# Holding back the preparation of weights until the first token tile is normalised: at three layer-norm boundaries the run-ahead of a weight queue gets a limit

## The chip, the cores and the metric

One core of a Trainium2 chip runs the whole kernel. The metric is the device time of one execution in microseconds; the figure quoted is the median of several runs. The engines are TensorE (PE, the matrix products; PEld its weight loads), VectorE (DVE), ScalarE (ACT), GpSimd (POOL) and SyncE (SP, which here only issues DMAs). Each engine works through its own list of instructions in order and waits at an instruction until the semaphores that it names have been reached.

## The reference

A decoder block of one layer works on 256 tokens of width 2048: a SwiGLU feed-forward net (width 5632), a mixer (recurrence plus attention), a second SwiGLU net, and a gated projection of per-layer embeddings. Behind each of the first three parts stands a residual and a layer norm over the 2048 columns of a token.

```python
def swiglu(x, w_gate, w_up, w_down):
    return (jax.nn.silu(x @ w_gate) * (x @ w_up)) @ w_down

x = layer_norm(ALPHA * x + 0.5 * swiglu(x, ffn1...), ln1_g, ln1_b)
x = layer_norm(ALPHA * x + hybrid_mixer(x, ...),     ln2_g, ln2_b)   # mixer: ... @ w_out
x = layer_norm(ALPHA * x + 0.5 * swiglu(x, ffn2...), ln3_g, ln3_b)
x = x + sigmoid(x @ w_ple_gate) * (p @ w_ple_proj)
```

All matrices are float32, so every weight passes through the core once, in 413 MB of transfers.

## The kernel before, in words

**Weights as entries of a plan.** A list `plan` holds all weights in the order of use, as entries of 256 rows by 512 columns (512 KB). An entry goes through three steps. SP loads it into a tile `raw` (10 buffers). ACT rounds it to a high part `hi` (line 104). DVE subtracts to get the low part `lo` (line 109). A product is then three passes on TensorE: act-high by hi, act-high by lo, act-low by hi.

**Where hi and lo live.** Most entries use the pools `whi` and `wlo` of 7 buffers each. An entry with `"work": True` takes both its tiles from the common pool `work` of 11 buffers (names `w4_...`, shown as `w` in the profile), which also holds activations. Such entries are the third and fourth of the eight that end each of the three parts (`last_down`), and the first three of the part that follows. At the end of a part the pool holds the two halves of the activations (2 tiles), the third and fourth entries (4 tiles), and what of the next part's first three entries is prepared (up to 6 tiles). In front of the third boundary one more tile holds the split per-layer embeddings.

**What sets the order.** `take()` hands out the next entry and lets `advance()` prepare further ones, up to 7 ahead (`AHEAD`), at most to `self.limit`, and only while fewer than 7 slots (`SLOTS`) of `whi` are in use; entries in the work pool don't count. `advance_lo` lets the subtractions lag the casts by one entry. `done(e)` gives a slot back and calls `advance()` again. No scheduler reorders anything within an engine: the order in which Python makes these calls is the order on each engine. Semaphores are added where a buffer is written again, so an instruction that needs a buffer waits for its last reader.

**The boundary.** `down_last` is the end of each part; it runs three times, at about 690, 1061 and 1770 us. It makes the last four column groups of 512 columns for the first token tile (tokens 0 to 127, below t0), two entries each. DVE adds each bank to `acc` (line 385) and takes its statistics (line 513). `ln_norm` then joins the statistics (lines 518 and 520), lets GpSimd take the inverse root (line 522), and scales the four column groups (line 525). The same four column groups follow for the second token tile (t1) with the same eight entries. In the middle of its second group, after 18 of the 48 matmuls of t1, stand the first transposes of the normalised t0 (`ln_transpose`, line 535). They are followed by ACT (lines 538 and 64) and DVE (line 65), which make the next part's activations `xT`. The next part starts with t0 for eight entries, and the transposes of t1 stand inside that.

**Names.** Below, the three calls are boundary I, II and III. The eight entries of `down_last` are e0 to e7 (e2 and e3 in the work pool). The entries of the next part are v0, v1, v2 (work pool), v3, and so on.

Of the kernel before, what the change touches and what calls it, by code (L numbers as in the profile page):

```python
# [40 lines left out]
class Block:  # L41
# [449 lines left out]

    def down_last(self, acts):
        es, st = [], [self.tile(self.small, [P, 4, 6], F32, "bst") for _ in range(2)]
        for n in range(4):
            es.append([self.take(), self.take()])
            self.down_mm(acts, es[n], 0, n, False)
            self.ln_stats(st[0], 0, n)
        self.ln_norm(st[0], 0)
        for n in range(4):
            self.down_mm(acts, es[n], 1, n, False, mid=(lambda: self.ln_transpose(0, 0)) if n == 1 else None)  # L500
            self.ln_stats(st[1], 1, n)
            if n < 3:
                for e in es[n]:
                    self.done(e)
            if n > 0:
                self.ln_transpose(0, n)
        self.ln_norm(st[1], 1)
        for e in es[3]:
            self.done(e)
# [499 lines left out]
```

## Time and profile before

| | us |
|---|---|
| median of 3 runs (1910.5 to 1912.78) | 1912.32 |
| the profiled execution's own time | 1905.79 |
| its span, first to last instruction | 1904.0 |
| PE busy | 1868.5 (98%) |
| DVE busy | 1494.9 (79%) |
| ACT busy | 1077.8 (57%) |

The profiled execution is another one than the three timed, and 6.5 us shorter than their median. PE is busy nearly all the time, so what can be won lies in the short stretches in which it stands still or runs at a lower clock. The page averages over stages; a boundary of some 20 us does not show in it, and has to be looked up in the timeline.

### The profile page before, as it was taken

The numbers are of one execution on the slowest core, as the hardware profiler recorded it, in microseconds if no ns is written. First come the engines' busy times: TensorE is split into PE (matmuls) and PEld (weight loads), VectorE is DVE, ScalarE is ACT, GpSimd is POOL, SyncE is SP. The second block draws the span as 40 slices with busy tenths as digits, with TensorE's granted clock in tenths as the row PEclk, the third lists the DMA queues.
The fourth block names the chain that finished last, engine by engine and source line by source line (L and its number), as shares of the span: only waits on it lengthen the run. The fifth ranks groups of instructions, "written<-read, shape, count | busy, mean of one in ns | idle before, by whom it ended". The sixth has DMA issues, their size and how long they took to land.

```text
span 1904.0 us, 26424 instructions
## 1 busy us (share of the span) xinstructions
PE 1868.5 (98%) x9844; PEld 1603.2 (84%) x9844; DVE 1494.9 (79%) x1910; ACT 1077.8 (57%) x1422; POOL 124.2 (7%) x108
## 2 busy tenths in 40 slices
PE   8999999999999989999999899999999999999899
PEld 7888888888888878887888788888888888888687
DVE  6698887887888876688677867878879888788674
ACT  6565555555655646555755455655556556556552
POOL 0001010100010000011100000101000101010000
PEclk9999999999999999999999999999999999999999
DMA  9678687788786857565455575887887878778381
GB/s 354 232 198 264 203 257 235 207 260 247 211 255 209 266 178 231 175 185 158 138 184 187 167 243 155 250 231 211 258 247 207 255 211 253 243 198 276 131 263 44
DMA packets 214593, 413.02 MB, mean 217 GB/s; under 512 B 13104, under 2 KB 15808, under 8 KB 214464
## 3 DMA queue, kind: packets, MB, share of 16 engines
q1 hardware_dynamic: 193856, 370.42, 58.1%
q0 software_dynamic: 20608, 40.91, 12.6%
q8 instruction: 77, 1.26, 0.3%
q14 instruction: 52, 0.43, 0.1%
HBM read 409.18 MB, written 2.10 MB: 216 GB/s over the span
## 4 chain that ended last, share of the span: by engine, by line
PE 95%; DVE 2%; ACT 1%; issue 1%; DMA 0%; SPq 0%; POOL 0%; DVEq 0%; POOLq 0%; ACTq 0%
PE mm L264 94%; DVE lo L109 1%; PE mm L535 1%; DMA raw<-in_ffn_w_gate_dram 0%; ACT hi L104 0%; DVE w L109 0%; DVE bst L513 0%; DVE acc L385 0%; PE mm L792 0%; DVE raw L82 0%; DVE w L721 0%; DVE w L65 0%; ACT w L64 0%; POOL rs L522 0%; DVE w L627 0%
## 5 line engine op out<-in xcount | busy, mean ns | idle before, releaser
L104 ACT CAST hi<-raw 128x1024 fp32r<-128x1024 f32 (+1 forms) x774 | 797.2, 1049 | 556.4 <-PE mm L264 501.2
L264 PE MATMUL mm<-xT,hi 128*128 128x512 f32 x3072 | 1057.6, 391 | 5.6 <-ACT hi L104 5.6
L109 DVE TENSOR_TENSOR lo<-raw,hi 128x1024 fp32r<-128x1024 f32 (+1 forms) x774 | 915.2, 1221 | 93.4 <-ACT hi L104 84.5
L264 PE MATMUL mm<-xT,lo 128*128 128x256 f32 x3072 | 850.5, 277 | 0.1
L264 PEld LDWEIGHTS mm<-xT,hi 128*128 128x128 f32 x3072 | 577.5, 188 | 127.2 <-ACT hi L104 5.8
L264 PEld LDWEIGHTS mm<-xT,lo 128*128 128x128 f32 x3072 | 577.7, 188 | 6.3 <-DVE lo L109 1.3
L264 PE MATMUL mm<-hi,w 128*128 128x512 f32 x1480 | 481.6, 391 | 1.8 <-DVE acc L435 1.2
L264 PEld LDWEIGHTS mm<-hi,w 128*128 128x128 f32 x1480 | 277.9, 188 | 63.7 <-ACT hi L104 1.5
L264 PE MATMUL mm<-lo,w 128*128 128x512 f32 x740 | 289.5, 391 | 0.0
L264 PE MATMUL mm<-hi,xT 128*128 128x512 f32 (+1 forms) x648 | 200.9, 385 | 0.0
L264 PEld LDWEIGHTS mm<-lo,w 128*128 128x128 f32 x740 | 139.1, 188 | 23.9
L85 POOL DMA_DIRECT2D raw<-in_ffn_w_down_dram x72 | 86.6, 1214 | 1080.7 <-DVE raw L82 547.7
L437 DVE TENSOR_TENSOR acc<-acc,mm 128x512 f32<-128x512 f32 x110 | 75.2, 684 | 98.6 <-PE mm L264 98.6
L264 PEld LDWEIGHTS mm<-hi,xT 128*128 128x128 f32 x648 | 120.3, 188 | 23.1
L264 PE MATMUL mm<-lo,xT 128*128 128x512 f32 (+1 forms) x324 | 123.6, 382 | 0.0
L378 DVE TENSOR_TENSOR w<-mm,w 128x256 f32<-128x256 f32 x192 | 80.2, 419 | 20.5 <-ACT w L377 20.0
L82 DVE TENSOR_TENSOR raw<-raw,raw 128x1024 f32<-128x1024 f32 x72 | 87.9, 1221 | 1.2
L377 ACT COPY w<-mm 128x256 f32<-128x256 f32 x192 | 69.6, 364 | 21.2 <-PE mm L264 17.2
L64 ACT CAST w<-qk 128x512 fp32r<-128x512 f32 (+1 forms) x42 | 25.5, 609 | 86.4 <-DVE qk L482 46.0
L612 ACT ACTIVATE w<-w 128x256 f32<-128x256 f32 x84 | 35.1, 418 | 66.3 <-DVE w L378 66.3
L264 PEld LDWEIGHTS mm<-lo,xT 128*128 128x128 f32 x324 | 61.0, 188 | 11.2
L613 DVE TENSOR_TENSOR w<-w,w 128x256 f32<-128x256 f32 x84 | 35.8, 426 | 41.4 <-ACT w L612 41.4
(139 smaller groups left out, 788.0 us busy)
## 6 DMA issues: line engine op xcount, KB each, us to landing
raw<-in_ffn_w_up_dram SPq DMA_DIRECT2D x176, 512.0 KB, 4.9
raw<-in_ffn_w_down_dram SPq DMA_DIRECT2D x176, 512.0 KB, 5.3
raw<-in_ffn_w_gate_dram SPq DMA_DIRECT2D x175, 512.0 KB, 6.0
raw<-in_w_in_dram SPq DMA_DIRECT2D x88, 512.0 KB, 4.6
raw<-in_ffn_w_down_dram POOLq DMA_DIRECT2D x72, 512.0 KB, 7.6
raw<-in_w_out_dram SPq DMA_DIRECT2D x32, 512.0 KB, 4.4
raw<-in_w_ple_gate_dram SPq DMA_DIRECT2D x32, 512.0 KB, 5.6
w<-in_ln_g_dram SPq DMA_DIRECT2D x12, 256.0 KB, 7.4
```

The lines of the kernel that those rows point to most:

```text
L64: self.nc.scalar.copy(hi, src)
L82: self.nc.vector.tensor_tensor(a, a, b, op=ALU.add)
L85: self.nc.gpsimd.dma_start(a, src, accum_op=ALU.add)
L104: self.nc.scalar.copy(e["hi"][:, k, :], e["raw"][:, k, :])
L109: self.nc.vector.tensor_tensor(e["lo"][:, k, :], e["raw"][:, k, :], e["hi"][:, k, :].bitcast(F32), op=ALU.subtract)
L264: self.nc.tensor.matmul(out, lhsT=lhsT, rhs=rhs, start=start, stop=stop, skip_group_check=True)
L377: self.nc.scalar.copy(c, bank[:, 256:])
L378: self.nc.vector.tensor_tensor(dst, bank[:, :256], c, op=ALU.add)
L437: self.nc.vector.tensor_tensor(a, a, bank, op=op)
L535: nc.tensor.transpose(bank[:, q * P:(q + 1) * P], self.acc[:, t, kb * P:(kb + 1) * P], self.ident)
L612: nc.scalar.activation(s, g, AF.Sigmoid)
L613: nc.vector.tensor_tensor(g, g, s, op=ALU.mult)
```

## The change

`down_last` sets the limit of the run-ahead to its own eight entries and two more before the first token tile, and lifts it again behind that tile's `ln_norm`. All other code stays.

```diff
     def down_last(self, acts):
         es, st = [], [self.tile(self.small, [P, 4, 6], F32, "bst") for _ in range(2)]
+        self.limit = self.taken + 10
         for n in range(4):
             es.append([self.take(), self.take()])
             self.down_mm(acts, es[n], 0, n, False)
             self.ln_stats(st[0], 0, n)
         self.ln_norm(st[0], 0)
+        self.limit = len(self.plan)
         for n in range(4):
             self.down_mm(acts, es[n], 1, n, False, mid=...)
             self.ln_stats(st[1], 1, n)
             if n < 3:
                 for e in es[n]:
                     self.done(e)
```

After the limit is lifted, the next call of `advance()` is the one in `done` behind the first column group of t1. The instructions of PE, ACT, SP and POOL stand in the same order as before, apart from buffer numbers. Only on DVE do some move, in the same way at each boundary. Place 1 is DVE at boundary I, from the statistics of the first column group to those of the last (`mm` are the four banks of t0, `w4_1283`, `w4_1287` and `w4_1290` the low parts of v0, v1 and v2). Before:

```order
L513 BN_STATS bst_1276_6561<-acc_85 128x6 [waits DVE_49]
L109 TENSOR_TENSOR w4_1283_6572<-raw_1267_6505,w4_1282_6571 128x1024 [waits DMAHW3_49,Activation_49]
L109 TENSOR_TENSOR w4_1287_6593<-raw_1270_6523,w4_1286_6592 128x1024 [waits DMAHW4_49,Activation_49]
L385 TENSOR_TENSOR acc_85<-acc_85,mm_1291_6602 128x512 [waits PE_49]
L513 BN_STATS bst_1276_6561<-acc_85 128x6 [waits DVE_49]
L109 TENSOR_TENSOR w4_1290_6599<-raw_1273_6541,w4_1289_6598 128x1024 [waits DMAHW5_49,PE_49,Activation_49]
L385 TENSOR_TENSOR acc_85<-acc_85,mm_1295_6623 128x512
L513 BN_STATS bst_1276_6561<-acc_85 128x6 [waits DVE_49]
L385 TENSOR_TENSOR acc_85<-acc_85,mm_1296_6638 128x512
L513 BN_STATS bst_1276_6561<-acc_85 128x6 [waits DVE_49]
```

The same place with the change (two lines were added, so lines behind 494 carry higher numbers):

```order
L515 BN_STATS bst_1276_6561<-acc_85 128x6 [waits DVE_49]
L109 TENSOR_TENSOR w4_1283_6572<-raw_1267_6505,w4_1282_6571 128x1024 [waits DMAHW3_49,Activation_49]
L385 TENSOR_TENSOR acc_85<-acc_85,mm_1288_6596 128x512 [waits PE_49]
L515 BN_STATS bst_1276_6561<-acc_85 128x6 [waits DVE_49]
L385 TENSOR_TENSOR acc_85<-acc_85,mm_1289_6611 128x512 [waits PE_49]
L515 BN_STATS bst_1276_6561<-acc_85 128x6 [waits DVE_49]
L385 TENSOR_TENSOR acc_85<-acc_85,mm_1290_6626 128x512 [waits PE_49]
L515 BN_STATS bst_1276_6561<-acc_85 128x6 [waits DVE_49]
```

The subtractions for v1 and v2 are gone from it. The one for v2 was the one that waits for PE.

Place 2 is DVE at boundary I behind the normalisation of t0, from the addition of t1's first bank to the first low part of `xT`. Before:

```order
L385 TENSOR_TENSOR acc_85<-acc_85,mm_1300_6663 128x512
L513 BN_STATS bst_1277_6562<-acc_85 128x6 [waits DVE_49]
L109 TENSOR_TENSOR lo_1294_6620<-raw_1278_6563,hi_1293_6619 128x1024 [waits DMAHW6_49,Activation_49]
L109 TENSOR_TENSOR lo_1303_6681<-raw_1281_6569,hi_1302_6680 128x1024 [waits DMAHW7_49,Activation_49]
L65 TENSOR_TENSOR xT_84<-qk_1309_6698,xT_84 128x4x128 [waits Activation_49]
```

The same place with the change:

```order
L385 TENSOR_TENSOR acc_85<-acc_85,mm_1294_6651 128x512 [waits PE_49]
L515 BN_STATS bst_1277_6562<-acc_85 128x6 [waits DVE_49]
L109 TENSOR_TENSOR w4_1287_6593<-raw_1270_6523,w4_1286_6592 128x1024 [waits DMAHW4_49,Activation_49]
L109 TENSOR_TENSOR w4_1297_6669<-raw_1273_6541,w4_1296_6668 128x1024 [waits DMAHW5_49,PE_49,Activation_49]
L109 TENSOR_TENSOR lo_1300_6675<-raw_1278_6563,hi_1299_6674 128x1024 [waits DMAHW6_49,Activation_49]
L109 TENSOR_TENSOR lo_1303_6681<-raw_1281_6569,hi_1302_6680 128x1024 [waits DMAHW7_49,Activation_49]
L67 TENSOR_TENSOR xT_84<-qk_1309_6698,xT_84 128x4x128 [waits Activation_49]
```

The two subtractions now stand here, ahead of those for v3 and v4 and of the first low part of `xT`.

Place 3 is PE at boundary I in t1's second column group, the same before and after. `w4_1260` and `w4_1261` are hi and lo of e2; the last row is the first transpose.

```order
L264 MATMUL mm_1307_6690<-w4_1260_6467,w4_1192_6125 128x512
L264 MATMUL mm_1307_6690<-w4_1261_6468,w4_1192_6125 128x512
L264 MATMUL mm_1307_6690<-w4_1260_6467,w4_1193_6126 128x512
L264 MATMUL mm_1307_6690<-w4_1260_6467,w4_1192_6125 128x512
L264 MATMUL mm_1307_6690<-w4_1261_6468,w4_1192_6125 128x512
L264 MATMUL mm_1307_6690<-w4_1260_6467,w4_1193_6126 128x512
L535 MATMUL mm_1308_6697<-ident_86,acc_85 128x128 [waits DVE_49]
```

Nothing moved here. The fifth row is the last reader of `w4_1261`; it is this matmul that the subtraction for v2 waits for, before and after, as its own low part takes that buffer.

## Rows read from the trace of the kernel before

**Rows 1.** Waits over the whole span: total us, times, longest

```profile
DVE w L109 <- PE mm L264: 13.2, 2, 6.9
PE mm L535 <- DVE acc L525: 19.1, 3, 8.0
```

**Rows 2.** Timeline of PE, boundary I: start us, us, instructions, idle before

```profile
688.63 2.88 PE L264 MATMUL mm<-w,w 128*128 128x512 f32 x12
...
699.51 1.52 PE L264 MATMUL mm<-w,w 128*128 128x512 f32 x6
706.62 1.11 PE L535 MATMUL mm<-ident,acc 128*128 128x128 f32 x4 [5.59 <-DVE acc L525]
```

**Rows 3.** The same of PE, boundary II

```profile
1070.25 1.52 PE L264 MATMUL mm<-w,w 128*128 128x512 f32 x6
1077.26 1.11 PE L535 MATMUL mm<-ident,acc 128*128 128x128 f32 x4 [5.49 <-DVE acc L525]
```

**Rows 4.** Timeline of PE, boundary III

```profile
1779.25 1.52 PE L264 MATMUL mm<-w,w 128*128 128x512 f32 x6
1788.80 1.11 PE L535 MATMUL mm<-ident,acc 128*128 128x128 f32 x4 [8.03 <-DVE acc L525]
```

**Rows 5.** Timeline of DVE, boundary I

```profile
690.31 2.34 DVE L109 TENSOR_TENSOR w<-raw,w 128x1024 fp32r<-128x1024 f32 x2
692.57 0.68 DVE L385 TENSOR_TENSOR acc<-acc,mm 128x512 f32<-128x512 f32 x1
...
700.90 1.23 DVE L109 TENSOR_TENSOR w<-raw,w 128x1024 fp32r<-128x1024 f32 x1 [6.92 <-PE mm L264]
...
703.37 0.67 DVE L385 TENSOR_TENSOR acc<-acc,mm 128x512 f32<-128x512 f32 x1
...
706.01 1.92 DVE L525 TENSOR_SCALAR acc<-acc,mv,rs 128x512 f32<-128x512 f32 x4 [0.76 <-POOL rs L522]
...
719.22 0.69 DVE L65 TENSOR_TENSOR xT<-qk,xT 128x512 fp32r<-128x512 f32 x1 [0.81 <-ACT xT L64]
...
720.94 1.92 DVE L525 TENSOR_SCALAR acc<-acc,mv,rs 128x512 f32<-128x512 f32 x4 [0.67 <-POOL rs L522]
```

**Rows 6.** Timeline of DVE, boundary III

```profile
1780.64 1.23 DVE L109 TENSOR_TENSOR w<-raw,w 128x1024 fp32r<-128x1024 f32 x1 [8.71 <-ACT hi L104]
```

**Rows 7.** Timeline of ACT, boundary III

```profile
1764.70 2.94 ACT L104 CAST w<-raw 128x1024 fp32r<-128x1024 f32 x3
```

**Rows 8.** PE by stretch, boundary I: us, busy (instructions), granted clock, DMA, GB/s

```profile
706.60:707.70 1.10, 1.08 (x5) 0.50 0.00 0
707.70:710.15 2.45, 2.45 (x9) 0.56 0.00 0
710.15:713.00 2.85, 2.85 (x16) 1.00 0.43 125
```

**Rows 9.** Chain that ended last, boundary I: start us, us, what

```profile
707.73 2.42 PE mm L264 x6
710.15 0.44 PE mm L535 x4
...
723.83 0.44 PE mm L535 x4
724.27 1.39 PE mm L264 x6
```

**Rows 10.** The same chain, boundary II

```profile
1078.38 2.56 PE mm L264 x6
1080.94 0.85 PE mm L535 x4
```

**Rows 11.** The same chain, boundary III

```profile
1789.91 2.35 PE mm L264 x6
```

**Rows 12.** DMA issues, 680 to 740 us: line, engine, times, KB, median us to landing

```profile
raw<-in_w_in_dram SPq DMA_DIRECT2D x16, 512.0 KB, 4.5
```

**Rows 13.** Engines by stretch, attention stage: PE, PEld, DVE, ACT, POOL, clock

```profile
889.00:896.30 7.30, 5.94 (x29) 4.52 (x27) 6.21 (x22) 4.30 (x6) 0.00 (x0) 1.00 0.50 144
```

## The prediction

> **What bounds the kernel now.** PE is busy for 98% of the span, as the table of the page shows, and no other engine comes near. A saving can only come from places where PE stands still. I therefore read the list of waits first, and in it the line in which PE itself waits: the transposes (line 535) waited for the scaling on DVE (line 525) three times, 19.1 us in all, the longest time 8.0 [rows 1]. Three times is once per boundary. The timeline of PE shows the places: 5.59 us at boundary I, 5.49 at II, 8.03 at III [rows 2, 3, 4].
>
> Next comes the question why DVE is late. At boundary I, DVE does the subtractions for v0 and v1, then the addition of t0's second bank, and then stands for 6.92 us in front of one subtraction, which starts at 700.90 [rows 5]. The row says that it waited for PE. The order says for which matmul: the last reader of e2's low part, the fifth of the six that start at 699.51 [rows 2], because the work pool has 11 tiles and v2's low part would be the twelfth. Those six are the last matmuls in front of the transposes. So PE has to finish them before DVE may go on, and then waits until DVE has added two banks, taken their statistics and scaled. The banks that DVE left lying were long complete: 48 matmuls run from 688.63 to 699.51, which is 0.227 us each, so t0's third bank was complete at about 694.2 and its fourth at 696.95 (36 matmuls after 688.63, plus 0.16 because the last one is 0.39 long).
>
> At III one more tile sits in the pool, so it is already v1's subtraction that waits. Its row names ACT [rows 6], but its cast is the second of the three that ran from 1764.70 on [rows 7]. The start at 1780.64 fits PE again: the six matmuls that start at 1779.25 [rows 4] give 1779.25 + 6 x 0.227 = 1780.61. Here three banks are left behind the waiting instruction, which explains the longer gap.
>
> Third, the clock. After the gap PE runs at a granted clock of 0.50 to 0.56 for 3.55 us, half speed being 1.2 GHz, and at 1.00 from 710.15 on [rows 8]. The first four transposes take 1.11 us instead of 0.44, and the six matmuls behind them 2.42 instead of 1.39 [rows 2, 9].
>
> **The change, part by part.** The limit takes the subtractions for v1 and v2 out of the stretch in front of the normalisation and puts them behind t1's first statistics. Casts, loads, matmuls and POOL's list keep their places.
>
> *Is the gap closed?* From the addition of t0's last bank to the first transposes the chain took 706.62 - 703.37 = 3.25 us [rows 2, 5]. With nothing in front of it, that addition can start when the bank is complete, at 696.95, since v0's subtraction (1.13 of the 2.34 us) and the two earlier additions fit between the banks, which come every 2.72 us. The transposes are then ready at 700.20. PE reaches them at 699.51 + 6 x 0.227 = 700.87. So PE arrives 0.67 us after they are ready and does not wait. At II and III the same 18 matmuls stand between the last bank of t0 and the transposes, 18 x 0.227 = 4.08 us against 0.16 + 3.25 = 3.41, so the margin is again 0.67.
>
> *What goes.* Boundary I: the wait 5.59, the slow transposes 1.11 - 0.44 = 0.67, the slow matmuls 2.42 - 1.39 = 1.03; together 7.29 [rows 2, 9]. Boundary II: 5.49, 0.67, 2.56 - 1.39 = 1.17, and a second slow group of transposes, 0.85 - 0.44 = 0.41; together 7.74 [rows 3, 10]. Boundary III: 8.03, 0.67, 2.35 - 1.39 = 0.96; together 9.66 [rows 4, 11]. Sum 24.69 us.
>
> *What is late next.* The two subtractions, 2.26 us as they follow each other (692.57 - 690.31) [rows 5], now stand between t1's first statistics and the first low part of xT. Behind them are queued v3's and v4's subtractions, xT, three additions and statistics of t1, and t1's scaling. The one who waits for the last is PE, at the first transposes of t1. Before, DVE took 720.94 - 706.01 = 14.93 us from scaling to scaling, of which 0.81 was idle waiting for ACT [rows 5]. With the two more and without that idle time it is 14.93 - 0.81 + 2.26 = 16.38. The first scaling now starts at 700.20 - 0.61 = 699.59, the second at 715.97, and the transposes can start at 716.58 (0.61 later, as 706.01 to 706.62). PE took 723.83 - 706.62 = 17.21 us from the first transposes of t0 to those of t1 [rows 2, 9]; without the slow 1.70 it is 15.51, which brings it there at 716.38. That is 0.2 us too early. Nearly all cover is used up here: each further microsecond on DVE between the two scalings would be a microsecond of PE. I charge 0.2 at I and the same at II. At III the 48 matmuls of the embeddings' projection stand in between (some 11 us), so nothing is charged. A new wait of 0 to 0.6 per boundary is possible; the sum takes 0.4 for all.
>
> *The other waits of the moved pieces.* v2's subtraction still waits for e2's last reader, 700.7 or so, but it now comes at about 704, when that is past. The first product with v1 comes behind all of t1, some 10 us after the first transposes, when v1's subtraction is long done. The raw buffers of v1 and v2 come free later, v1's at about 704 instead of 692.6; SP's list is in order, so the tenth load behind v1's moves with it and the loads behind that line up. They land 4.5 us after issue [rows 12], at about 709. The entry that this load brings is v11. The next part starts 30 matmuls and four groups of transposes after 700.87, at about 709.5, and spends 96 matmuls (21.8 us) on its first eight entries, so v11 is wanted after 731. That is 22 us of cover, so I cost it at nothing.
>
> *Sum.* 24.69 - 0.4 = 24.3 us from the profiled 1905.79 gives 1881.5. The median of the timed runs lies 6.53 above the profiled execution, and I carry that over: 1888.0.
>
> **A rule weighed.** In [rows 5] DVE did not take the addition behind the waiting subtraction, though its bank was complete six microseconds before. The Trainium skill ("TensorE: Matmul & The Clock Gate", the section on architectural detail) says that the queues of ACT and DVE are strictly first in, first out. The trace agrees. The rule speaks against the change as well: whatever is put behind the normalisation delays all that follows it on DVE, and by the rule alone the result would be the first rival's 1894.4.
>
> **The rivals.** *First, DVE's lateness comes back behind the boundary.* If DVE had no cover after the first scaling, the 2.26 us would reach PE at each boundary in place of the 0.4 charged: 3 x 2.26 = 6.8, so 1888.0 + 6.8 - 0.4 = 1894.4. For it: the cover at I is used up to 0.2 us. Against it: the 0.81 idle and the shorter PE path are counted above from rows. If the clock also fell again at each of these waits (1.70 as at I) it would be 1899.5. Against that stands a stretch in which PE stood for 7.30 - 5.94 = 1.36 us in pieces and the clock stayed at 1.00 [rows 13]. The Trainium skill, on the same page ("What's actually happening"), has the throttled clock as the default that activity releases; by it too short waits cost only themselves.
>
> *Second, only the moved work is saved.* If something other than that wait holds DVE up to 700.9 (PE's record may name the wrong releaser), the gain is the 2.26 us per boundary that stand in front: 6.8, so 1905.5. Against it: at I and III the start of the waiting subtraction matches the end of the sixth matmul to 0.1 us, and the order names that reader.
>
> *Third, slower: the weights come late.* The place is SP's list behind the load that waits for v1's raw buffer. It would decide once that load landed later than 731, 27 us after its issue in place of 4.5; then PE would wait for v11 at each boundary. To end slower, over 28 us must go there, 9.4 per boundary, as 24.3 are gained and 3.8 is the bound of what can be told. The time would be 1916 or more. The DMA engines are idle in part at the boundary (share 0.43 from 710 to 713 [rows 8]), so nothing speaks for it.
>
> *Fourth, nothing changes*, because another wait of the same length takes the place: 1912. The rows show none.
>
> **How the numbers follow.** My forecast has 0.81, the first rival 0.10, the second 0.04, the third 0.03, the fourth 0.02. What a measurement of this kernel can tell from no change is 0.2%, 3.8 us. The forecast and the first two rivals lie beyond it, so faster has 0.95, the same 0.02 and slower 0.03. The range goes from 1885.5 (no new wait at all, and 2 us of the runs' own spread) to 1896, which takes in the first rival.
>
> **What would show it.** Right: in the changed profile DVE no longer waits for PE in front of a line 109 between t0's additions; PE has no wait over 1 us at the first transposes of t0; the granted clock stays at 1.00 across the boundary; PE's busy time falls by some 5 us through the clock and its idle time by some 19. Wrong: a wait of PE for line 525 or line 65 of over 1 us at the transposes of t1, a drop of the clock there, or ACT waiting for transfers of the entries v9 to v13.

## The result, and the profile after

| | before | after |
|---|---|---|
| median of the timed runs | 1911.41 (1909.25 to 1912.78, 4 runs) | 1884.49 (1883.24 to 1885.79, 4 runs) |
| the profiled execution's own time | 1905.79 | 1883.24 |
| its span | 1904.0 | 1881.5 |
| PE busy | 1868.5 | 1864.6 |

The ratio is 0.986, with a 95% interval from 0.9843 to 0.9877: faster by 27 us (23.5 to 30). The forecast was 1888.0, with a range from 1885.5 to 1896. The time lies below that range by 1.0 us. The four runs after include the profiled execution; the four before do not include theirs, which was shorter than all of them.

The engine table of the profile after (busy us, share of the span, instructions):

```profile
PE 1864.6 (99%) x9844; PEld 1601.1 (85%) x9844; DVE 1494.1 (79%) x1910; ACT 1077.3 (57%) x1422; POOL 124.2 (7%) x108
```

PE's idle time in the span fell from 35.5 to 16.9 us, by 18.6; the terms for it in the prediction were 5.59 + 5.49 + 8.03 - 0.4 = 18.7. Its busy time fell by 3.9 us instead of the 5.58 of the slow transposes and matmuls; the difference is explained further down.

The timeline of DVE after, boundary I (start us, us, instruction; in brackets the idle time ahead of it and what ended it), answers to [rows 5]:

```profile
690.80 1.21 DVE L109 TENSOR_TENSOR w<-raw,w 128x1024 fp32r<-128x1024 f32 x1
...
694.75 0.69 DVE L385 TENSOR_TENSOR acc<-acc,mm 128x512 f32<-128x512 f32 x1 [1.31 <-PE mm L264]
...
697.47 0.69 DVE L385 TENSOR_TENSOR acc<-acc,mm 128x512 f32<-128x512 f32 x1 [1.30 <-PE mm L264]
...
700.14 1.92 DVE L527 TENSOR_SCALAR acc<-acc,mv,rs 128x512 f32<-128x512 f32 x4 [0.76 <-POOL rs L524]
...
703.29 2.34 DVE L109 TENSOR_TENSOR w<-raw,w 128x1024 fp32r<-128x1024 f32 x2
...
716.42 1.92 DVE L527 TENSOR_SCALAR acc<-acc,mv,rs 128x512 f32<-128x512 f32 x4 [0.67 <-POOL rs L524]
```

Only v0's subtraction is left in front. The last two additions now wait 1.31 and 1.30 us for their own banks, as they should, and nothing waits 6.92 us any more. The subtractions for v1 and v2 run at 703.29 without a wait. From scaling to scaling DVE takes 716.42 - 700.14 = 16.28 us; the prediction worked out 16.38.

The chain that ended last, after, at the three boundaries (start us, us, what) answers to [rows 9, 10, 11]. The row of 580.97 us is PE's unbroken stretch up to boundary I:

```profile
120.55 580.97 PE mm L264 x3102
701.52 0.44 PE mm L537 x4
701.96 1.39 PE mm L264 x6
...
717.03 0.66 PE mm L537 x4
...
1065.26 0.44 PE mm L537 x4
...
1080.78 0.55 PE mm L537 x4
...
1767.90 0.44 PE mm L537 x4
1768.34 1.39 PE mm L264 x6
...
1794.29 0.44 PE mm L537 x4
```

The chain stays on PE through each boundary. The first transposes of t0 take 0.44 us and the six matmuls behind them 1.39, the values at full clock; before they were 1.11 and up to 2.56. The first transposes of t1 show what new wait there is: 0.66 - 0.44 = 0.22 us at I, 0.11 at II, none at III. The prediction charged 0.2, 0.2 and 0.

PE by stretch, after (us, busy and instructions of PE, PEld, DVE, ACT and POOL, granted clock, DMA share, GB/s) answers to [rows 8]:

```profile
680.00:700.90 20.90, 20.90 (x93) 17.29 (x93) 13.01 (x19) 7.67 (x8) 0.57 (x1) 1.00 0.56 193
700.90:703.30 2.40, 2.40 (x15) 1.96 (x14) 2.37 (x6) 1.66 (x5) 0.00 (x0) 1.00 0.00 0
1767.30:1771.00 3.70, 3.70 (x22) 3.09 (x21) 3.67 (x7) 2.92 (x8) 0.00 (x0) 1.00 0.00 0
```

PE is busy all the time across the boundary, and the granted clock stays at 1.00.

To compare stages, the span is cut at four marks of the chain: S, the start of the unbroken stretch of PE that leads to boundary I, and T1, T2, T3, the first transposes of t0 at the three boundaries. "Predicted" takes the prediction's terms out of the profile of before, each in the stage in which it falls (behind T1, for example, lie the slow 1.70 of I, the wait 5.49 of II and the new wait of 0.2):

| | start to S | S to T1 | T1 to T2 | T2 to T3 | T3 to the end |
|---|---|---|---|---|---|
| before | 120.06 | 586.56 | 370.64 | 711.54 | 115.20 |
| predicted | 120.06 | 580.97 | 363.65 | 701.46 | 113.57 |
| after | 120.55 | 580.97 | 363.74 | 702.64 | 113.60 |

Three stages meet the working within 0.1 us. One is 1.2 us too long, the start is 0.5 us longer, and so the profiled executions alone give 22.6 us, while the medians differ by 27. The experiments had to settle two things: whether the mechanism is the one named, and where the difference between profiles and medians comes from.

### The profile page after: what moved, and what is told of

It is laid out like the page before. It is cut to its first block, busy times and chain, and to the rows that moved or that the text cites. A ratio compares the mean times of both kernels' runs of the same rounds, so it can differ in the third digit from the quotient of the medians.

```text
span 1881.5 us, 26424 instructions
## 1 busy us (share of the span) xinstructions
PE 1864.6 (99%) x9844; PEld 1601.1 (85%) x9844; DVE 1494.1 (79%) x1910; ACT 1077.3 (57%) x1422; POOL 124.2 (7%) x108
## 4 chain that ended last, share of the span: by engine, by line
PE 96%; DVE 2%; ACT 1%; issue 1%; DMA 0%; SPq 0%; ACTq 0%; DVEq 0%
PE mm L264 95%; DVE lo L109 1%; PE mm L537 1%; ACT hi L104 0%; DMA raw<-in_ffn_w_gate_dram 0%; PE mm L794 0%; DVE w L378 0%; DMA raw<-in_ffn_w_down_dram 0%; DVE raw L82 0%; DVE w L723 0%; DVE w L65 0%; ACT w L64 0%; ACT w L614 0%; DVE w L629 0%; DVE w L615 0%
```

## The experiments

The theory that went into them is the prediction's: DVE stands in front of a subtraction whose low part would be the twelfth tile of the work pool, PE waits for the scaling behind it, and the clock falls in the gap. The rivals were that only the moved work counts, that DVE is merely late, and, for the missed size, that the executions of before differ among themselves (by the granted clock, theory C, or by the start of the program, theory S). The first four were run together in 5 rounds beside 16 runs of the kernel before (median 1910.52, 1906.74 to 1913.09), the next four in 3 rounds beside 13 (1909.50, 1906.67 to 1910.91).

**The two kernels again**, unchanged.

> The kernel before, once more, to see how its executions differ. Open is why its timed runs (1909.25 to 1912.78) lie 3.5 to 7 us above its profiled one (1905.79), while the changed kernel's profiled run lies among its timed ones. Theory C (clock): after each boundary's gap PE runs at the lower clock for a time that differs from execution to execution; then the mean granted clock is lower in the longer runs: 0.995 at 1905.8, about 0.992 at 1911 (a loss of 5 us is 10 us at half speed, 10/1904 = 0.005, of which half or more stands behind the gaps), and a profile of a 1911 us run shows line 535's first transposes of t0 and the matmuls behind them slow for longer than the 3.55 us of boundary I. Theory E (elsewhere): the mean clock is 0.995 whatever the time, and the extra time lies in stages away from the boundaries. Median expected 1909 to 1913 by both.

> The changed kernel once more, for the size of the gain. Theory C: its runs stay within 1883 to 1886 with a mean clock of 0.999 to 1.000, as there is no gap left for the clock to fall in; ratio 0.985 to 0.987. Theory E: its runs spread as widely as those of the kernel before.

Measured: 1910.79 (11 runs, ratio 1.0004, 0.9995 to 1.0013) and 1883.14 (4 runs, 0.9866, 0.985 to 0.9881). The gain holds. The runs of the change spread over 5.0 us (1881.52 to 1886.47) at a mean clock of 0.999 to 1.000, wider than theory C allowed and almost as wide as the 5.5 of the 11 runs. The 1912.32 that the prediction started from is at the upper end of what the kernel before does.

**The clock alone.** Dummy matmuls into a spare bank fill PE's gap at each boundary; the wait of DVE stays.

```diff
+FILL = (23, 23, 34)
+        def first():
+            scratch = self.bank()
+            for q in range(FILL[self.which]):
+                self.mm(scratch, acts[0][:, q % 4, :P], es[3][1]["hi"][:, q % 2, :], True, True)
+            self.ln_transpose(0, 0)
```

> The kernel before, with matmuls whose results nobody reads put in front of the first transposes of t0: 23 at boundary I and II, 34 at III (0.227 us each, 5.2 and 7.7 us), on the high part of the last entry. They lie in the gaps of 5.59, 5.49 and 8.03 us. DVE's wait and the gap stay; only the clock should not fall. Theory C: the slow transposes and matmuls behind the gap become as fast as elsewhere, 1.70, 2.25 and 1.63 us by the profile of before and more in the timed runs; median 1911.4 - 5.6 - 5 = about 1901, spread as narrow as the changed kernel's, clock 0.999 or more. Theory E: only the 5.6 us of the profile go, median about 1906, and the spread stays. If the clock has no part in it: 1911.

Measured: 1904.53 (6 runs), ratio 0.997 (0.9958 to 0.9981), so 6.0 us less than before (3.6 to 8.0). PE at boundary I by stretch, first the dummies, then from the end of the gap on, same columns as above:

```profile
701.60:707.10 5.50, 5.42 (x24) 4.14 (x23) 4.52 (x8) 0.00 (x0) 0.57 (x1) 1.00 0.32 95
707.10:710.00 2.90, 2.60 (x16) 2.25 (x17) 2.87 (x7) 1.88 (x5) 0.00 (x0) 1.00 0.02 6
```

The chain at the same place:

```profile
707.40 0.66 PE mm L543 x4
708.05 1.39 PE mm L265 x6
```

S to T1 stays at 586.56, as in before to the hundredth, since the dummies only take the place of the idle time. The clock stays at 1.00 and the six matmuls take 1.39 in place of 2.42. By the prediction's terms this is worth 1.70 + 2.25 + 1.63 = 5.58 us, less three waits of 0.22 for the scaling. The clock is thus a loss of its own, nearly a quarter of the whole, and comes from PE's gap. Theory C had asked for 5 us more, 1901; they did not come. The runs do spread less (1902.9 to 1904.96), but 1904.53 lies nearer to theory E's 1906, so the distance of the timed runs from the profile is not, in the main, the clock behind the gaps.

**One entry more.** The limit at 11: v1 is prepared in front of the normalisation again, v2 not.

```diff
-        self.limit = self.taken + 10
+        self.limit = self.taken + 11
```

> The changed kernel with the limit at three entries behind the boundary in place of two. v1's subtraction then stays in front of the normalisation and only v2's moves behind it, at all three boundaries. Theory T (the wait for the work pool's twelfth tile is what costs): at I and II it is v2's subtraction that waits, so the gaps of 5.59 and 5.49 us and the slow clock behind them go; at III it is v1's that waits, so its gap of about 8 us less 1.2 (v2's subtraction no longer stands in it) stays. Gain by the profile of before 7.3 + 7.7 + 1.2 = 16, about 1894 in the timed runs, and line 109 waits once, at III only, for 8.7 us. Rival M (only the moved subtractions count): 1.13 us at each of three boundaries, 1908, all three boundaries alike.

Measured: 1893.6 (4 runs), ratio 0.9912 (0.9899 to 0.9926), 10.5 above the change. This is the run that names the pool. At I and II eleven tiles are enough without v2, and the gap is gone. At III, with one tile more in the pool, the twelfth is v1's low part. DVE there:

```profile
1769.25 1.23 DVE L109 TENSOR_TENSOR w<-raw,w 128x1024 fp32r<-128x1024 f32 x1 [8.70 <-ACT hi L104]
```

and PE at I and III:

```profile
703.19 0.60 PE L537 MATMUL mm<-ident,acc 128*128 128x128 f32 x4
...
1767.86 1.52 PE L264 MATMUL mm<-w,w 128*128 128x512 f32 x6
1776.26 1.11 PE L537 MATMUL mm<-ident,acc 128*128 128x128 f32 x4 [6.88 <-DVE acc L527]
```

At III the subtraction starts at 1767.86 + 6 x 0.227 = 1769.22, when e2's low part has been read for the last time, as in [rows 4, 6]. Its row names ACT, as there, but the start is PE's. One subtraction moved in front of a boundary costs nothing at I and II, and at III 6.88 us of wait and 1.9 of slow clock, so the work itself is not what mattered.

**No limit, but more room.** First the order of before with 13 tiles in the work pool; two of the ten raw buffers make the space. The second kernel has the eight raw buffers alone.

```diff
-RAWS = 10
+RAWS = 8
-            tc.tile_pool(name="work", bufs=11) as self.work,
+            tc.tile_pool(name="work", bufs=13) as self.work,
```

> The order of the kernel before, with 13 tiles in the work pool in place of 11, so that v1's and v2's low parts find a free tile at every boundary; all subtractions stay in front of the normalisation. To make room there are 8 raw buffers in place of 10, whose own effect the next run shows. Theory T (the wait costs, not the moved work): the three gaps go as with the change, since two subtractions of 1.13 us fit between banks that come every 2.72 us; 24 to 27 us below the kernel with 8 raw buffers and 11 tiles. Rival M (the moved work costs): no gain, as nothing is moved.

> The kernel before with 8 raw buffers in place of 10 and nothing else, as the comparison for the run with 13 tiles. Loads run less far ahead: 1911 if they have cover, some us more if not. The three gaps at the boundaries stay (5.6, 5.5, 8.0 us).

Measured: 1887.54 (4 runs), ratio 0.9885 (0.9868 to 0.9901), and 1911.64 (10 runs), 1.001 (1.0001 to 1.002), with all three gaps as before (5.58, 5.49 and 8.02 us). Two tiles more, without any change of order, are worth 24.1 us. DVE at boundary I with 13 tiles:

```profile
699.11 1.21 DVE L109 TENSOR_TENSOR w<-raw,w 128x1024 fp32r<-128x1024 f32 x1
...
704.87 1.92 DVE L525 TENSOR_SCALAR acc<-acc,mv,rs 128x512 f32<-128x512 f32 x4 [0.76 <-POOL rs L522]
...
718.88 2.06 DVE L525 TENSOR_SCALAR acc<-acc,mv,rs 128x512 f32<-128x512 f32 x4 [0.67 <-POOL rs L522]
```

v2's subtraction stands where it stood before and waits for nothing, and all three gaps are gone. The rival that only the moved work is saved falls with this: nothing was moved, and the gain is the same. The Trainium skill ("Perfetto Trace Analysis", the section "Optimization Strategy") says that a gap that repeats on the engine that should be busy can mean that there is no room for the next tile. These two runs agree, with 24.1 us for two tiles; here the engine with the gap (PE) is another than the one that lacks the tile (DVE).

**No limit, but one entry less in the pool.** Of the next part's entries only v0 and v1 are work entries; v2 uses the other pools.

```diff
-            for e in plan[q:q + 3]:
+            for e in plan[q:q + 2]:
```

> The kernel before without the limit, but with only the first two entries of the next part in the work pool (v2 goes to the seventh slot of the hi and lo pools). The work pool then never wants a twelfth tile. v1's subtraction stays in front of the normalisation. Theory T: all three gaps go, III too, in contrast to the limit of eleven entries, which has the same order on DVE there; about 1884. If what matters is which subtractions stand in front, it ends like the limit of eleven, 1893.6.

Measured: 1884.55 (4 runs), ratio 0.987 (0.9855 to 0.9884). It can't be told from the change. DVE's two subtractions in front of boundary III, v0's and v1's:

```profile
1758.01 2.35 DVE L109 TENSOR_TENSOR w<-raw,w 128x1024 fp32r<-128x1024 f32 x2
```

The same two stood there with the limit at 11, where the second waited 8.70 us. With one entry less in the pool it does not wait, and the gap at III is gone too. So it is the tile that counts, and not what stands in front. DVE's two scalings at I:

```profile
700.64 1.92 DVE L525 TENSOR_SCALAR acc<-acc,mv,rs 128x512 f32<-128x512 f32 x4 [0.76 <-POOL rs L522]
...
715.80 2.06 DVE L525 TENSOR_SCALAR acc<-acc,mv,rs 128x512 f32<-128x512 f32 x4 [0.67 <-POOL rs L522]
```

**One entry less.** The limit at 9: three subtractions are moved behind the normalisation.

```diff
-        self.limit = self.taken + 10
+        self.limit = self.taken + 9
```

> The changed kernel with the limit at one entry behind the boundary: v0's subtraction too moves behind the normalisation, so three subtractions stand between it and the first low part of xT. By the cover worked out for the change (DVE 16.38 us from scaling to scaling against 15.5 of PE, a wait of 0.2 measured as 0.22) a further 1.13 us on DVE is a further 1.1 us of wait at I and II at the first transposes of t1, and none at III: 1.3 us there in each, about 1885.5 in all. If DVE had cover left, 1883.

Measured: 1886.65 (4 runs), ratio 0.988 (0.9865 to 0.9894), 2.1 above the run with two work entries on the same chip. PE at the first transposes of t1, boundaries I and II (no wait at III):

```profile
720.16 0.66 PE L537 MATMUL mm<-ident,acc 128*128 128x128 f32 x4 [1.15 <-DVE acc L527]
...
1084.90 0.66 PE L537 MATMUL mm<-ident,acc 128*128 128x128 f32 x4 [1.04 <-DVE acc L527]
```

From scaling to scaling DVE takes 14.01 us with 13 tiles, 15.16 with two work entries, 16.28 with the change and 17.42 with the limit at 9: one subtraction, 1.14 on average, per step. PE begins to wait at the third of these (0.22 us) and waits 1.15 at the fourth. So the cover was indeed used up to 0.2 us, as the prediction had it. The first rival, by which the change itself pays 2.26 per boundary, did not happen, and its mechanism begins one entry further on.

**More executions**: the kernel before four times on one chip, then the change four times on another, each with a profile.

> A further execution of the kernel before, for its profile. Of 27 timed executions, 20 had a mean granted clock of 0.993 or 0.994 and took 1911.1 us on average, and 7 had 0.995 or 0.996 and took 1908.0. Both profiles so far are of the second kind (0.995, 0.996). Theory C: an execution of the first kind shows, behind at least one of the three gaps, line 535's transposes and the matmuls behind them slow for longer than the 3.4 to 3.6 us in the profiles so far, by 3 to 4 us more in all. Theory S: the difference lies in the first 125 us, where PE reaches its unbroken stretch at 120.1 in one profile and 123.7 in the other; behind that all executions agree to 0.5 us.

> As the look before: by theory C the sum over the three gaps of the time at the lower clock sets the execution's time, by theory S the first 125 us.

> As the two looks before, a further draw: theory C asks for a longer slow stretch behind a gap in a longer execution, theory S for a longer start.

> As the three looks before, a further draw: theory C asks for a longer slow stretch behind a gap in a longer execution, theory S for a longer start.

> A further execution of the changed kernel, for its profile. In six executions of the kernel before, PE reached its unbroken stretch at 120.06 to 123.66, half of them above 122.4; in two of the changed one at 120.55 and 120.20. If the draws were only few, further executions spread over 120 to 123.7 too. If the change shortens the start, all stay below 121.2. The stages between the boundaries are expected at 580.97, 363.7, 701.3 or 702.6, and 113.6 by both.

> A further draw of the changed kernel: few draws ask for starts up to 123.7 among the four looks, a real difference for starts below 121.2 in all.

> A further draw of the changed kernel: few draws ask for starts up to 123.7 among the four looks, a real difference for starts below 121.2 in all.

> A further draw of the changed kernel: few draws ask for starts up to 123.7 among the four looks, a real difference for starts below 121.2 in all.

With the two first profiles and the two of the first experiment this makes six executions of either kernel with a trace. S to T1 (586.56 to 586.59, and 580.95 to 580.99) and T1 to T2 (370.48 to 370.71, and 363.60 to 363.74) hardly vary. Two stages do, in both kernels. S comes either at 120.1 to 120.6 us or at 122.4 to 123.7. T2 to T3 takes either the short value (711.4 to 711.5 before, 701.3 after) or about 1.4 us more. In before, the two executions with this step also lost 0.9 us more to the low clock at III. Five of the six executions of before start late (the expectation speaks of half), and three of the six of the change. As four more draws of the change gave three late starts, the change can't be said to shorten the start. Sorted by these two, the times of the profiled executions are:

| start | step | before | after | difference |
|---|---|---|---|---|
| early | no | 1905.79 | 1881.52 | 24.3 |
| early | yes | none | 1883.24, 1883.02 | |
| late | no | 1909.16, 1908.08, 1908.04 | 1884.34 | 24.1 |
| late | yes | 1910.47, 1911.15 | 1885.69, 1886.04 | 24.9 |

The sorting was made after the times were known. But the marks are read from the traces, not from the times, and like against like gives the same difference three times, but for the 0.9 us at III that the 24.9 holds. The two late rows compare executions on different chips; the two stages that hardly vary agree across them to 0.04 and 0.23 us. Theory S holds for the larger part, a start that is 2.8 us longer on average in either kernel, but not in that all executions agree behind it. Theory C (lower clock) holds only for 0.9 us at III in two of six.

What lies behind both marks, at the start for the larger part, is PE's own pace. PE by stretch, late start (the kernel before, second profile):

```profile
40.00:72.00 32.00, 32.00 (x183) 27.82 (x182) 17.88 (x21) 12.82 (x15) 0.00 (x0) 1.00 0.86 303
```

early start (the change, second profile):

```profile
40.00:72.00 32.00, 32.00 (x190) 28.37 (x189) 18.94 (x22) 13.54 (x17) 0.00 (x0) 1.00 0.91 319
```

In both PE is busy for all 32 us at a granted clock of 1.00, but it puts through 190 matmuls in the one and 183 in the other. The transfers differ here too (319 and 303 GB/s), but they are not what sets the pace. Earlier in the same two executions, late start first, they are alike, and PE puts through 171 matmuls and 178:

```profile
20.00:50.00 30.00, 30.00 (x171) 26.13 (x170) 20.83 (x24) 18.89 (x25) 0.00 (x0) 1.00 1.05 386
20.00:50.00 30.00, 30.00 (x178) 26.63 (x177) 21.90 (x25) 19.54 (x26) 0.00 (x0) 1.00 1.05 387
```

The same in the stretch behind boundary II, with two executions of the change. The additions that follow every twelve matmuls, with the step:

```profile
1128.10 0.69 DVE L567 TENSOR_TENSOR acc<-acc,w 128x512 f32<-128x512 f32 x1
1130.90 0.69 DVE L565 TENSOR_TENSOR acc<-acc,w 128x512 f32<-128x512 f32 x1
1133.70 0.69 DVE L567 TENSOR_TENSOR acc<-acc,w 128x512 f32<-128x512 f32 x1
```

and without it:

```profile
1127.67 0.68 DVE L567 TENSOR_TENSOR acc<-acc,w 128x512 f32<-128x512 f32 x1
1130.39 0.69 DVE L565 TENSOR_TENSOR acc<-acc,w 128x512 f32<-128x512 f32 x1
1133.11 0.68 DVE L567 TENSOR_TENSOR acc<-acc,w 128x512 f32<-128x512 f32 x1
```

They come every 2.80 us in the one and every 2.72 in the other, 3% apart. What makes PE take the slower pace in some executions is open.

## Why the prediction was right, and where it was wrong

**The gap.** Right. The wait in front of the twelfth tile is shown from three sides: one subtraction back brings the gap back at III alone, where the pool holds one tile more; two tiles more remove it with the order of before; one work entry less removes it too, at III with the very subtractions in front that stood there with the limit at 11.

**PE arrives behind the scaling.** Right. PE runs through the first transposes of t0 at all three boundaries.

**The clock.** Right. With the gap filled and DVE's wait kept, the clock stayed at 1.00, and the gain was 6.0 us (3.6 to 8.0) for a term of 5.58 less 0.66.

**What is late next.** Right. 16.28 us from scaling to scaling for 16.38, and waits of 0.22, 0.11 and 0 for 0.2, 0.2 and 0. Without a drop of the clock there: the chain shows the matmuls behind these waits at 1.38 and 1.39 us.

**The weights behind v1.** Right that they cost nothing. PE's stage behind boundary I came out at 363.74 for 363.65, so there is no place in it for a wait for v11.

**PE's busy time.** Predicted to fall by some 5 us, measured 3.9. The profiled execution after has the slower pace of PE behind boundary II, which puts 1.36 us into the busy time; without it the fall would be 5.3.

**The sum.** 24.3 us was predicted. Like against like the profiles give 24.3, 24.1 and 24.9, and the means over the six profiled executions of either kernel, 1908.78 and 1883.98, give 24.8. "1905.79 gives 1881.5" was met by the one execution of the change with early start and no step, at 1881.52. The timed medians lie 27 us apart (23.5 to 30), within whose uncertainty 24.3 to 24.9 fits. Whether the last 2 us of that are a different mixture in the timed runs is not shown, since these leave no trace; but each has its mean granted clock. Of the six profiled executions of before, the two with the step and the 0.9 us at III have 0.993 and 0.994, the other four 0.995 or 0.996. Of the 27 runs of before in the first round of experiments (16 and 11), 20 have 0.993 or 0.994 (1911.1 us on average) and 7 have more (1908.0); the 13 on another chip all have 0.995 or 0.996 (median 1909.50). So in that round most runs seem to be of the longer kind, while the profile that the prediction started from, with 0.995, was of the shorter. The start leaves no such mark.

**The step that failed** is the last sentence of the sum: "The median of the timed runs lies 6.53 above the profiled execution, and I carry that over: 1888.0." The 6.53 is no property of the kernel. The profiled execution of before was the shortest of all that were seen, with early start and no step, and the median of three timed runs was at the upper end: 11, 13 and 16 more runs of the same kernel have medians of 1910.79, 1909.50 and 1910.52. In the profiled execution after, start and pace had fallen differently, and the median lies 1.25 above it. The carry-over was thus mis-sized by 5.3 us, and the forecast missed by 3.5, as that execution itself lay 1.7 above 1881.5 through its longer T2 to T3 and its later S. The range inherited it: its low end allowed for "2 us of the runs' own spread", where the offset itself was uncertain by several. That one profiled execution stood 4.7 us below the lowest of three timed runs, whose own spread was 2.3, was the visible sign that the offset varies. A low end at the profiled sum, 1881.5, would have held the time.

No version that was tried beats the change by what can be measured; two work entries in place of three do the same without a limit.

## What to carry to other kernels

Where an engine works in order, a buffer pool that is one tile short can stop it at an instruction whose buffer is read by work that stands later in the program, and another engine then pays; to see it, compare the start of the waiting instruction with the end of the buffer's last reader, and test it with one more buffer or one piece less. Before work is moved behind a boundary, count the slack there in units of that work: here it was two subtractions to within 0.2 us, and the third cost 1.0 to 1.2 us at two of the three boundaries. Work out a gain within one trace, and treat the distance between one profiled execution and the median of the timed runs as noise of its own, with both ends kept for the range.

## What was not expected of the hardware

PE does not have one pace at a granted clock of 1.00. With PE busy all the time, twelve matmuls took 2.72 us behind boundary II in one execution of the change and 2.80 in another, and in the twelve traces the stretch from 40 to 72 us holds 189 to 191 matmuls or 183 to 185. A pace holds evenly for tens of microseconds, differs between executions of the same kernel, and is worth 1.4 us at the one place and 2 to 3 at the other. The records of the clock don't show it, only the spacing of the instructions.
